# A two-layer DeltaNet/Conformer encoder on one core: gate tiles two ahead, splits two to a place, transposes in groups 1-2-1, the scan's last parts and the merge's operands in another order

## The chip, the core and the metric

The kernel runs on one NeuronCore of a Trainium2 chip. Five engines take part, each with its own instruction stream: TensorE (PE, matmuls and transposes into PSUM), VectorE (DVE, elementwise on PSUM and SBUF), ScalarE (ACT, functions by table, copies, squares), GpSimd (POOL) and SyncE (SP, which issues most DMAs; ACT and POOL issue some). [...] The metric is the time on the device of one launch, in microseconds (us), as the median of several runs; less is better.

## The reference

Two layers, each on x of 2048 tokens x 1024 channels (float32), then a final RMSNorm:

```
h = rms_norm(x, norm_w)
qkv, z_a, a_lg, b_lg, cf_val, cf_glu, z_b, gate_lg = split(h @ w_in)
q, k, v = silu(depthwise_conv5(qkv));  q, k = l2_normalize(q), l2_normalize(k)      # 4 heads of 128
o = delta_rule(q, k, v, g, beta) + flip(delta_rule(flip(q), ...))                   # 2 directions
o = o * rsqrt(mean(o*o) + EPS) * dn_norm_w * silu(z_a);  y_a = o @ w_dn_out
u = silu(layer_norm(depthwise_conv31(cf_val * sigmoid(cf_glu)) + cf_conv_b)) * silu(z_b)
y_b = u @ w_cf_out
gate = sigmoid(gate_lg + gate_b)                       # one gate of 1024 for each branch
x = x + (gate[0] * y_a + gate[1] * y_b) @ w_out
```

The delta rule is a scan in chunks: in each chunk a small triangular system, and from chunk to chunk a 128x128 state for each head and direction.

## The kernel before

Activations lie with channels on the 128 partitions and tokens along the free dimension. The 2048 tokens are four blocks of 512 (`blk` 0 to 3), two to a half. Every projection is made of denses: one output tile of 128 channels x 512 tokens in a PSUM bank (`pd`). Weights and operands are cut in a high and a low part by `split` (L158 on ACT copies the high part, L159 on DVE subtracts), and `dense_steps` (L175 to L177) runs three matmuls of 512 columns for each 128 input channels: 24 matmuls where the input has 1024 channels (w_in, w_out), 12 where it has 512 (w_cf, w_dn). Small results go to the five banks of `pz`.

A layer runs in four stages.

**Projections and heads.** `conv_tiles` makes the denses of two or three 128-channel columns of w_in and a five-tap convolution with SiLU (L546) for each half. Work that hangs on it is put in queues as Python generators and taken up between denses: `follow` lets a generator of `post` go on to its next `yield` after each dense, and `pump` does the same for `back` by a credit in us (a `yield 0.0` ends the pump for this dense). `keys` is a `post` generator: `token_major` turns 16 chunks of 128 tokens with PE transposes (L567), four to a pz bank and eight between two yields, the keys first, then the queries; ACT squares them (L595, L605) and copies the keys (L597). Then come the gram products of 16 chunks (L622, L623), copied by ACT (L625). `conformer_conv` is a 31-tap convolution on DVE (L734), a `back` generator, and `conformer_norm` (another, one for each blk) is the layer norm of branch B: sums over channels by PE, squares, a sum for each token (`token_sum`, L201), a reciprocal root, and a multiply. The string `Z` says how many empty pumps lie between its parts.

**Scan.** `delta` walks 16 steps, chunk `step` forward and chunk 15 - `step` backward in one pass, first half of the steps storing o, second half adding to it and closing the chunk with `finish` (squares L1028, reciprocal root on DVE from L1038 to L1042, scale by ACT L1046, transposes by PE L1051, product with z_a L1052, store of og). Its matmuls are short, so it pulls denses from a filler between its parts: `pull(n)` takes n pieces of three matmuls. The filler is the second half's gate columns (`gates(1)`, 256 pieces), then `early_merge`: branch B's products of half 0 (w_cf, 12 matmuls each), multiplied by the sigmoid of a gate tile (`g`) into `y1`. The operand `u` is loaded and split (tile `uop`) at given pieces: `SPLIT` is the first of eight pieces in a row. After the loop, `TAIL` gives the pulls between the last parts of `finish`. The order of the scan is bound as written (`bind`) on PE, ACT, DVE and POOL; elsewhere the tile framework schedules each engine's stream by priority and buffers.

**Merge.** For each half, 8 output tiles j and two blocks b: `gt` (a gate tile, in an `hm` buffer; two gates in half 1) is loaded and put through a sigmoid (L1227); in half 1 a dense with wc (w_cf) gives branch B, multiplied with the gate (L1232); a dense with wd (w_dn) over `og` gives branch A (L1235), the two are added (L1236) and split into yhi and ylo. In half 0 the operand `og` (tile `gop`) is loaded in four pieces of 1024 tokens when the scan ends; half 1's operands are loaded during half 0's output projection.

**Output.** w_out over yhi and ylo, residual, next layer's norm; in the last layer `last_out` with the final norm.

Of the kernel before, what the change touches and what calls it, by code (L numbers as in the profile page):

```python
# [6 lines left out]
F32 = mybir.dt.float32  # L7
F32R = mybir.dt.float32r
# [6 lines left out]
P = 128  # L15
# [4 lines left out]
KD = 8  # L20
# [7 lines left out]
GAP = 0  # L28
SPLIT = 247
LEAD = (8, 10, 6, 6, 6, 4)  # L30
STEP = (4, 4, 4, 4)
TAIL = (3, 3, 2)
Z = '121'
# [25 lines left out]
def sort(ps):  # L59
    return ps.rearrange("p (i a) -> p a i", a=2)  # L60


def cut(x):
    return x.rearrange("p (a i) -> p a i", a=2)
# [13 lines left out]
class Trunk:  # L78
# [482 lines left out]

    def token_major(self, src, f):
        for q in range(4):
            ps = self.pz()
            for i in range(4):
                c = 4 * q + i
                self.nc.tensor.transpose(ps[:, i * P:(i + 1) * P], src[:, c * P:(c + 1) * P], self.ident)  # L567
            f(q, ps)
            if q % 2:
                yield  # L570
# [15 lines left out]
    def keys(self, hd, kt, qt, vs):  # L586
# [5 lines left out]
        def k_out(q, ps):  # L592
            ko = self.st("ko")
            for i in range(4):
# [4 lines left out]
                       ko.rearrange("p (c e) -> p c e", e=P))  # L599
        yield from self.token_major(kt, k_out)  # L600
        self.store(self.kq_d[:, :, hd, 1, :].rearrange("c p t -> p c t"), qt.rearrange("p (c t) -> p c t", t=P))
        ssq = self.sm(16, "ssq")
        def q_out(q, ps):
            for i in range(4):
                nc.scalar.activation(self.junk, ps[:, i * P:(i + 1) * P], AF.Square,  # L605
                                     accum_out=ssq[:, 4 * q + i:4 * q + i + 1])
        yield from self.token_major(qt, q_out)
        rq = self.sm(16, "rq")
# [140 lines left out]
    def conformer_norm(self, blk):  # L749
# [23 lines left out]
        yield 4.0  # L773
        for _ in range(int(Z[1])):
            yield 0.0
# [42 lines left out]
    def delta(self):  # L818
# [272 lines left out]
        for step in range(NCH):  # L1091
# [25 lines left out]
            new = finish(list(done))  # L1117
            done.clear()
            next(new)
            pull(STEP[2])  # L1120
# [4 lines left out]
            ins = nxt  # L1125
        for n in TAIL:
            pull(n)
            next(last)
        for _ in fill:
# [3 lines left out]
    def filler(self):  # L1133
        wcf = self.a["w_cf"][self.l]
        u = None
        for n, v in enumerate(self.gates(1)):
            yield v
            if n == 30 * KD - 1:
# [4 lines left out]
                for b in range(2):  # L1143
                    for k in range(4):
                        self.load(raw(k, b).bitcast(F32), self.u_d[k, :, b * NB:(b + 1) * NB])
            if n == 31 * KD - 1:
                ahead = self.weight(wcf[0], 4)
            if SPLIT <= n < SPLIT + 8:
                b, k = divmod(n - SPLIT, 4)
                self.split(u[:, k, b * NB:(b + 1) * NB], raw(k, b), raw(k, b).bitcast(F32))  # L1150
        self.u0 = u
        self.y1 = self.big([P, KD, HALF], F32, "y1")
        yield from self.early_merge(wcf, ahead)

    def early_merge(self, wcf, ahead):
        nc = self.nc
        seq = [(j, b) for j in range(KD) for b in range(2)]

        def gate(i):
            j, b = seq[i]  # L1160
            t = self.st("g1")
            self.load(t, self.gt_d[8 + j][:, b * NB:(b + 1) * NB])
            return t
        nxt = gate(0)
        for i, (j, b) in enumerate(seq):
            if b == 0:
                wc = ahead
                if j + 1 < KD:
                    ahead = self.weight(wcf[j + 1], 4)
            g = nxt  # L1170
            if i + 1 < len(seq):
                nxt = gate(i + 1)
            nc.scalar.activation(g, g, AF.Sigmoid)
# [26 lines left out]
    def merge(self, l, xd, fnw):  # L1200
# [10 lines left out]
        for half in range(2):  # L1211
            if half == 0:
                og, piece = self.operands(self.og_d, 0, "gop")
                for k in range(4):
                    piece(k)
            yhi = self.big([P, KD, HALF], F32R, "yhi")
            ylo = self.big([P, KD, HALF], F32R, "ylo")
            for j in range(KD):
                wc = self.weight(a["w_cf"][l, j], 4) if half else None
                wd = self.weight(a["w_dn"][l, j], 4)  # L1220
                for b in range(2):
                    sl = slice(b * NB, (b + 1) * NB)
                    tk = slice(half * HALF + b * NB, half * HALF + (b + 1) * NB)
# [3 lines left out]
                    nc.scalar.activation(gt[:, 0:n], gt[:, 0:n], AF.Sigmoid)  # L1227
                    y = [gt[:, 0, :], gt[:, 1, :] if half else self.y1[:, j, sl]]
                    if half:
                        ps = self.pd()  # L1230
                        self.dense(ps, wc, lambda k: (u[:, k, sl], u[:, 4 + k, sl]), 4)
                        v_.tensor_tensor(out=cut(y[1]), in0=sort(ps), in1=cut(y[1]), op=ALU.mult)  # L1232
                    ps = self.pd()
                    self.dense(ps, wd, lambda k: (og[:, k, sl], og[:, 4 + k, sl]), 4)
# [8 lines left out]
            if last:  # L1243
                self.last_out(l, half, xd, fnw, yhi, ylo, ahead)
                continue
# [3 lines left out]
            for j in range(KD):  # L1249
# [10 lines left out]
                if j == 0:  # L1260
                    ss = self.hm("ss")[:, 0:HALF]
                for b in range(2):
                    sl = slice(b * NB, (b + 1) * NB)
# [30 lines left out]

    def last_out(self, l, half, xd, fnw, yhi, ylo, ahead):
        nc, a = self.nc, self.a
# [40 lines left out]

        for b in range(2):
            o = b * NB
# [111 lines left out]
```

## Time and profile before

| | us |
|---|---|
| median of three runs | 3188.68 (3188.55 to 3192.41) |
| the profiled execution's own time | 3190.01 |
| its span in the trace | 3188.2 |
| stage: projections and heads of layer 0 | about 100 to 800 |
| scan of layer 0 | about 800 to 1300 |
| merge and output of layer 0 | about 1300 to 1700 |
| layer 1, the same stages | 1700 to 2400, 2400 to 2860, 2860 to 3188 |

The profile names an instruction by its engine, its line in the kernel (L567), its operation and its tiles (output<-inputs, buffer numbers left out), then partitions x elements. In a timeline a row gives start, duration, and in brackets how long the engine had been idle before it and what it had waited for. Rows of the same kind in sequence are merged (x7). Durations of matmuls overlap; from start to start they show the pace. PEclk is the clock granted to PE as a share of full speed. DMA rows with SPq, ACTq or POOLq tell who issued them.

### The profile page before, as it was taken

How to read it: one execution, taken by the hardware profiler on the slowest of the kernel's cores; microseconds unless marked ns; L12 is line 12 of the kernel's file. 1: busy time of each engine (PE TensorE's matmuls, PEld its weight loads, DVE VectorE, ACT ScalarE, POOL GpSimd, SP SyncE). 2: the span in 40 equal slices, each digit the busy share in tenths (PEclk: the TensorE clock that was granted, in tenths of full speed). 3: DMA queues.
4: the chain of work that ended last, by engine and by line, in shares of the span. 5: the costliest groups of instructions: out<-in, count | busy, mean ns of one | idle time of the engine just before them, and what ended most of it. 6: DMA issues, size and time to landing. Idle time of an engine off the chain costs nothing. (4 is left out here: it accounts for less than half of the span.)

```text
span 3188.2 us, 51447 instructions
## 1 busy us (share of the span) xinstructions
PE 3095.3 (97%) x19190; PEld 2712.7 (85%) x19190; DVE 2400.1 (75%) x4433; ACT 1385.1 (43%) x3107; POOL 301.4 (9%) x297
## 2 busy tenths in 40 slices
PE   6999999999999999999999999999999999999998
PEld 5788888888889998787888888888888899978787
DVE  7789898987656697745676989898954567867665
ACT  5625151522444466533345242425234445655342
POOL 3000000000022231000000000000001213200000
PEclk9999999999999999999999999999999999999999
DMA  4332232334687886554413131313357878855643
GB/s 140 89 97 93 85 95 85 96 110 132 204 287 251 256 263 212 189 189 128 141 50 108 66 115 65 114 66 113 125 169 261 260 240 259 282 185 190 207 152 126
DMA packets 428266, 501.72 MB, mean 157 GB/s; under 512 B 96304, under 2 KB 262832, under 8 KB 428016
## 3 DMA queue, kind: packets, MB, share of 16 engines
q1 hardware_dynamic: 354688, 388.58, 39.2%
q10 hardware_dynamic: 65264, 80.09, 7.3%
q0 software_dynamic: 8064, 29.76, 2.5%
q8 instruction: 151, 2.47, 0.3%
q14 instruction: 99, 0.81, 0.1%
HBM read 342.74 MB, written 155.58 MB: 156 GB/s over the span
## 5 line engine op out<-in xcount | busy, mean ns | idle before, releaser
L175 PE MATMUL pd<-h,whi 128*128 128x512 f32 x2816 | 1091.8, 388 | 0.0
L177 PE MATMUL pd<-h,wlo 128*128 128x512 f32 x2816 | 1070.2, 380 | 2.2 <-DVE wlo L159 2.2
L176 PE MATMUL pd<-h,whi 128*128 128x512 f32 x2816 | 1071.3, 380 | 0.0
L734 DVE SCALAR_TENSOR_TENSOR cacc<-gp,vec,cacc 128x1009 f32<-128x1009 f32 (+1 forms) x480 | 614.5, 1280 | 37.8 <-ACT cacc L732 34.6
L175 PEld LDWEIGHTS pd<-h,whi 128*128 128x128 f32 x2816 | 534.1, 190 | 79.3 <-issue 1.4
L177 PEld LDWEIGHTS pd<-h,wlo 128*128 128x128 f32 x2816 | 533.9, 190 | 79.2 <-DVE wlo L159 3.8
L176 PEld LDWEIGHTS pd<-h,whi 128*128 128x128 f32 x2816 | 534.2, 190 | 72.4 <-issue 1.9
L158 ACT ACTIVATE whi<-wraw 128x512 fp32r<-128x512 f32 x394 | 239.1, 623 | 451.0 <-PE pd L176 325.4
L159 DVE TENSOR_TENSOR wlo<-wraw,whi 128x512 fp32r<-128x512 f32 x394 | 272.1, 704 | 133.4 <-ACT whi L158 133.0
L559 DVE SCALAR_TENSOR_TENSOR acc<-cin,vec,acc 128x1022 f32<-128x1022 f32 (+1 forms) x192 | 246.6, 1299 | 14.4 <-ACT acc L557 13.2
L177 PE MATMUL pd<-yhi,wlo 128*128 128x512 f32 x488 | 185.7, 381 | 3.8 <-DVE wlo L159 3.8
L175 PE MATMUL pd<-yhi,whi 128*128 128x512 f32 x488 | 185.5, 380 | 1.2 <-ACT whi L158 1.2
L176 PE MATMUL pd<-ylo,whi 128*128 128x512 f32 x488 | 185.0, 379 | 0.0
L814 ACT ACTIVATE go<-pd,vec 128x512 f32<-128x512 f32 x128 | 87.0, 680 | 145.7 <-PE pd L177 136.2
L535 ACT ACTIVATE cin<-pd 128x512 f32<-128x512 f32 x96 | 56.9, 593 | 154.9 <-PE pd L177 154.8
L746 ACT ACTIVATE ao<-pd 128x512 f32<-128x512 f32 x64 | 38.3, 598 | 170.0 <-PE pd L177 169.9
L175 PE MATMUL pd<-uop,whi 128*128 128x512 f32 x256 | 102.2, 399 | 7.1 <-ACT whi L158 7.1
L177 PEld LDWEIGHTS pd<-yhi,wlo 128*128 128x128 f32 x488 | 92.2, 189 | 19.2 <-DVE wlo L159 6.2
L175 PEld LDWEIGHTS pd<-yhi,whi 128*128 128x128 f32 x488 | 92.2, 189 | 15.0 <-ACT whi L158 2.3
L176 PEld LDWEIGHTS pd<-ylo,whi 128*128 128x128 f32 x488 | 92.2, 189 | 12.9
L177 PE MATMUL pd<-uop,wlo 128*128 128x512 f32 x256 | 99.5, 389 | 2.4 <-DVE wlo L159 1.7
L176 PE MATMUL pd<-gop,whi 128*128 128x512 f32 x256 | 98.2, 384 | 2.4 <-DVE gop L159 2.3
(311 smaller groups left out, 4837.1 us busy)
## 6 DMA issues: line engine op xcount, KB each, us to landing
wraw<-w_in SPq DMA_DIRECT2D x240, 256.0 KB, 3.3
gt<-go ACTq DMA_DIRECT2D x128, 256.0 KB, 3.6
dl<-gr SPq DMA_DIRECT2D x128, 256.0 KB, 5.1
dl<-kq SPq DMA_DIRECT2D x64, 512.0 KB, 6.3
dl<-kv SPq DMA_DIRECT2D x64, 512.0 KB, 5.6
wraw<-w_out SPq DMA_DIRECT2D x90, 256.0 KB, 3.1
kq<-acc SPq DMA_DIRECT2D x16, 1024.0 KB, 5.4
gr<-go ACTq DMA_DIRECT2D x64, 256.0 KB, 2.2
```

What stands on the lines that cost most here:

```text
L158: self.nc.scalar.activation(hi, src, AF.Copy)
L159: self.nc.vector.tensor_tensor(out=lo, in0=src, in1=hi.bitcast(F32), op=ALU.subtract)
L175: mm(ps, whi[:, k, :], xhi, start=k == 0, stop=False)
L176: mm(ps, whi[:, k, :], xlo, start=False, stop=False)
L177: mm(ps, wlo[:, k, :], xhi, start=False, stop=k == kk - 1)
L535: nc.scalar.activation(cut(t[:, o + b * NB:o + (b + 1) * NB]), sort(ps), AF.Copy)
L559: self.nc.vector.scalar_tensor_tensor(out=out, in0=t[:, k:k + n], scalar=wc(k), in1=out, op0=ALU.mult, op1=ALU.add)
L734: self.nc.vector.scalar_tensor_tensor(out=acc, in0=t[:, k:k + n], scalar=wc(k), in1=acc, op0=ALU.mult, op1=ALU.add)
L746: nc.scalar.activation(cut(o), sort(ps), func)
L814: nc.scalar.activation(cut(o), sort(ps), AF.Identity, bias=self.vec[:, V_GB + j:V_GB + j + 1])
```

## The change

Seven edits, letters as they are used below.

- **A.** `token_major` takes the places of its yields as an argument; keys and queries yield after the first and third bank. The groups of the heads become [k0], [k1, k2], [k3, q0], [q1, q2], [q3 and the gram products of chunks 0 to 7], [gram, chunks 8 to 15], where they were [k0, k1], [k2, k3], [q0, q1], [q2, q3], [gram], [gram].
- **B.** One more empty pump before the token sum of blk 3 in `conformer_norm`.
- **C.** u's eight splits at pieces 245 to 258, two to a pull, in place of eight pieces from 247.
- **D.** The gate tiles of `early_merge`: two are loaded before it begins, and each round issues the load of the tile after next.
- **E.** The scan's last parts: the loop ends after the last squares, and the two open `finish` generators go on in the order new, last, new, new, new with 2, 2, 1, 3, 4 pieces ahead.
- **F.** og's half 0 in eight pieces of 512 tokens, block 1 first; the merge, w_out and `last_out` of half 0 take block 1 first.
- **G.** In half 1 of the merge, wc's denses of both blocks come before wd's of both; the gate tiles of both blocks are loaded and put through the sigmoid ahead.

```diff
-SPLIT = 247
+SPLITS = (245, 247, 249, 251, 253, 255, 257, 258)
-TAIL = (3, 3, 2)
+TAIL = (2, 2, 1, 3, 4)
...
-    def token_major(self, src, f):
+    def token_major(self, src, f, cuts=(1, 3)):
...
-            if q % 2:
+            if q in cuts:
                 yield
...
-        yield from self.token_major(kt, k_out)
+        yield from self.token_major(kt, k_out, (0, 2))
...
-        yield from self.token_major(qt, q_out)
+        yield from self.token_major(qt, q_out, (0, 2))
...
-        for _ in range(int(Z[1])):
+        for _ in range(int(Z[1]) + (blk == 3)):
             yield 0.0
...
             new = finish(list(done))
             done.clear()
+            if step == NCH - 1:
+                break
             next(new)
...
-        for n in TAIL:
+        for n, part in zip(TAIL, (new, last, new, new, new)):
             pull(n)
-            next(last)
+            next(part)
...
+        seq = [(j, b) for j in range(KD) for b in range(2)]
+        u = ahead = None
+        gs = deque()
+
+        def gate(i):
+            j, b = seq[i]
+            t = self.st("g1")
+            self.load(t, self.gt_d[8 + j][:, b * NB:(b + 1) * NB])
+            gs.append(t)
...
+                gate(0)
             if n == 31 * KD - 1:
                 ahead = self.weight(wcf[0], 4)
-            if SPLIT <= n < SPLIT + 8:
-                b, k = divmod(n - SPLIT, 4)
+                gate(1)
+            if n in SPLITS:
+                b, k = divmod(SPLITS.index(n), 4)
                 self.split(u[:, k, b * NB:(b + 1) * NB], raw(k, b), raw(k, b).bitcast(F32))
...
-            g = nxt
-            if i + 1 < len(seq):
-                nxt = gate(i + 1)
+            if i + 2 < len(seq):
+                gate(i + 2)
+            g = gs.popleft()
...
-                og, piece = self.operands(self.og_d, 0, "gop")
-                for k in range(4):
-                    piece(k)
+                og = self.big([P, 8, HALF], F32R, "gop")
+                for b in (1, 0):
+                    c = slice(b * NB, (b + 1) * NB)
+                    for k in range(4):
+                        self.load(og[:, 4 + k, c].bitcast(F32), self.og_d[k, :, c])
+                        self.split(og[:, k, c], og[:, 4 + k, c], og[:, 4 + k, c].bitcast(F32))
...
+            order = (0, 1) if half else (1, 0)
             for j in range(KD):
+                ys = {}
...
-                for b in range(2):
-                    sl = slice(b * NB, (b + 1) * NB)
+                for b in order:
...
-                    y = [gt[:, 0, :], gt[:, 1, :] if half else self.y1[:, j, sl]]
-                    if half:
+                    ys[b] = [gt[:, 0, :], gt[:, 1, :] if half else self.y1[:, j, b * NB:(b + 1) * NB]]
+                if half:
+                    for b in order:
+                        sl = slice(b * NB, (b + 1) * NB)
+                        y = ys[b]
                         ps = self.pd()
                         self.dense(ps, wc, lambda k: (u[:, k, sl], u[:, 4 + k, sl]), 4)
                         v_.tensor_tensor(out=cut(y[1]), in0=sort(ps), in1=cut(y[1]), op=ALU.mult)
+                for b in order:
+                    sl = slice(b * NB, (b + 1) * NB)
+                    y = ys[b]
                     ps = self.pd()
                     self.dense(ps, wd, lambda k: (og[:, k, sl], og[:, 4 + k, sl]), 4)
...
-                for b in range(2):
+                for b in order:
```

The lines of the kernel after this change are shifted: L1173, L1179, L1227, L1232, L1235 and L1236 of before are L1181, L1187, L1239, L1247, L1253 and L1254 after.

On PE, in the second head of layer 0, the transposes (L567) stand between matmuls of the values' denses. Before:

```order
L177 MATMUL pd<-h_107,wlo 128x512
L567 MATMUL pz<-con,acc 128x128 x7
L175 MATMUL pd<-h_231,whi 128x512
...
L175 MATMUL pd<-h_231,whi 128x512
L567 MATMUL pz<-con,acc 128x128
L176 MATMUL pd<-h_231,whi 128x512
```

Ten matmuls lie between the seventh transpose and the eighth, where the scheduler put it. After the change:

```order
L177 MATMUL pd<-h_107,wlo 128x512
L567 MATMUL pz<-con,acc 128x128 x4
L175 MATMUL pd<-h_231,whi 128x512
...
L177 MATMUL pd<-h_231,wlo 128x512
L567 MATMUL pz<-con,acc 128x128 x8
```

The first group ends after four, and the eighth transpose stands in the group one dense of 24 matmuls later.

On ACT, step 14 of the scan in layer 0: u's splits (uop), the squares and the first gates. Before:

```order
L158 ACTIVATE uop<-uop 128x512 x4
L814 ACTIVATE go<-pd,vec 128x512
L152 DMA gt_150<-go 128x512
L947 ACTIVATE dh_6989<-pz 128x256
L909 ACTIVATE dh_6988<-dh_6988 32x4x32 x4
L1028 ACTIVATE junk,oss<-dm_6984 128x128 x8
L158 ACTIVATE whi<-wraw 128x512
L1173 ACT_TABLE_LOAD
L1173 ACTIVATE g_11059<-g_11059 128x512
L1173 ACTIVATE g_11067<-g_11067 128x512
L982 ACTIVATE dm_6983<-pz,eg 128x128 x8
```

After:

```order
L158 ACTIVATE uop<-uop 128x512 x2
L814 ACTIVATE go<-pd,vec 128x512
L152 DMA gt_150<-go 128x512
L947 ACTIVATE dh_6989<-pz 128x256
L909 ACTIVATE dh_6988<-dh_6988 32x4x32 x4
L1028 ACTIVATE junk,oss<-dm_6984 128x128 x8
L158 ACTIVATE uop<-uop 128x512
L158 ACTIVATE whi<-wraw 128x512
L1181 ACT_TABLE_LOAD
L1181 ACTIVATE g_10748<-g_10748 128x512
L158 ACTIVATE uop<-uop 128x512 x2
L1181 ACTIVATE g_10896<-g_10896 128x512
```

Two of the four splits ahead of the squares are gone from there (they come a place earlier), and three that stood earlier still now lie behind the squares, two of them between the two gates.

On DVE, half 1 of the merge, one round of j. Before:

```order
L1232 TENSOR_TENSOR gt<-pd,gt 128x512
L159 TENSOR_TENSOR ylo<-gt,yhi 128x512
L159 TENSOR_TENSOR wlo<-wraw,whi 128x512
L1235 TENSOR_TENSOR gt<-pd,gt 128x512
L159 TENSOR_TENSOR wlo<-wraw,whi 128x512
L1236 TENSOR_TENSOR gt<-gt 128x512
L159 TENSOR_TENSOR ylo<-gt,yhi 128x512
L1232 TENSOR_TENSOR gt<-pd,gt 128x512
L1235 TENSOR_TENSOR gt<-pd,gt 128x512
L1236 TENSOR_TENSOR gt<-gt 128x512
```

After:

```order
L1247 TENSOR_TENSOR gt<-pd,gt 128x512 x2
L159 TENSOR_TENSOR wlo<-wraw,whi 128x512
L1253 TENSOR_TENSOR gt<-pd,gt 128x512
L1254 TENSOR_TENSOR gt<-gt 128x512
L159 TENSOR_TENSOR ylo<-gt,yhi 128x512
L1253 TENSOR_TENSOR gt<-pd,gt 128x512
L159 TENSOR_TENSOR wlo<-wraw,whi 128x512
L1254 TENSOR_TENSOR gt<-gt 128x512
L159 TENSOR_TENSOR ylo<-gt,yhi 128x512
```

The two subtractions of weights (wlo), which stood close together around one multiply, now stand four operations apart, and both multiplies of branch B come first.

More of the change, by code (lines that the diff above doesn't have):

```diff
@@ L1134, in filler, with units @@
         wcf = self.a["w_cf"][self.l]
-        u = None
-        for n, v in enumerate(self.gates(1)):
+        seq = [(j, b) for j in range(KD) for b in range(2)]
[6 more added lines that the diff above has]
+            gs.append(t)
+        def units():
+            yield from self.gates(1)
+            self.u0 = u
+            self.y1 = self.big([P, KD, HALF], F32, "y1")
+            yield from self.early_merge(wcf, ahead, seq, gs, gate)
+        for n, v in enumerate(units()):
             yield v
@@ L1145, in filler, with early_merge @@
                         self.load(raw(k, b).bitcast(F32), self.u_d[k, :, b * NB:(b + 1) * NB])
+                gate(0)
             if n == 31 * KD - 1:
                 ahead = self.weight(wcf[0], 4)
-            if SPLIT <= n < SPLIT + 8:
-                b, k = divmod(n - SPLIT, 4)
+                gate(1)
+            if n in SPLITS:
+                b, k = divmod(SPLITS.index(n), 4)
                 self.split(u[:, k, b * NB:(b + 1) * NB], raw(k, b), raw(k, b).bitcast(F32))
[L1151 to L1155, printed above, removed]
+    def early_merge(self, wcf, ahead, seq, gs, gate):
         nc = self.nc
[L1157 to L1164, printed above, removed]
         for i, (j, b) in enumerate(seq):
@@ L1243, in merge @@
             if last:
-                self.last_out(l, half, xd, fnw, yhi, ylo, ahead)
+                self.last_out(l, half, xd, fnw, yhi, ylo, ahead, order)
                 continue
@@ L1293, in late_norm, with last_out @@
         yield from self.normalise(1, xn, r, wcol)
-    def last_out(self, l, half, xd, fnw, yhi, ylo, ahead):
+    def last_out(self, l, half, xd, fnw, yhi, ylo, ahead, order):
         nc, a = self.nc, self.a
@@ L1336, in run @@
                     return
-        for b in range(2):
+        for b in order:
             o = b * NB
```

## The prediction

> **What bounds the kernel now.** First the busy times on the page of the profile:
>
> ```profile
> PE 3095.3 (97%) x19190; PEld 2712.7 (85%) x19190; DVE 2400.1 (75%) x4433; ACT 1385.1 (43%) x3107; POOL 301.4 (9%) x297
> ```
>
> TensorE (PE) is busy for 97% of the span, DVE for three quarters, ACT for less than half. The change removes no matmul, so all it can win or lose is time in which PE stands still or runs at a lower clock. The table of what PE waited for (total us, times, longest) says where that is:
>
> ```profile
> PE pz L567 <- ACT acc L546: 8.9, 6, 1.6
> PE pz L973 <- DVE dh L1052: 8.4, 2, 4.2
> PE pz L201 <- DVE lnt L772: 5.5, 4, 1.9
> PE pd L176 <- DVE gop L159: 2.3, 3, 0.8
> PE pz L1051 <- ACT dm L1046: 2.2, 2, 1.1
> PE pd L175 <- ACT gop L158: 1.0, 2, 0.8
> ```
>
> Most edits of the change stand beside one of these rows. A stall can cost more than its idle time. The table of windows (length; busy time and count of each engine; granted PE clock; DMA share; GB/s) shows stretches at half clock:
>
> ```profile
> 1235.60:1239.00 3.40, 2.46 (x11) 2.46 (x12) 3.35 (x8) 1.05 (x5) 1.27 (x1) 0.50 0.63 200
> 1303.90:1307.30 3.40, 3.27 (x8) 2.63 (x9) 3.40 (x5) 2.72 (x5) 0.00 (x0) 0.50 0.87 328
> 1454.10:1457.50 3.40, 3.40 (x8) 2.62 (x9) 2.70 (x6) 1.05 (x2) 0.00 (x0) 0.50 0.48 91
> 2420.00:2423.40 3.40, 3.40 (x9) 2.68 (x10) 2.74 (x16) 0.00 (x0) 0.00 (x0) 0.51 0.63 204
> 2846.70:2850.10 3.40, 3.40 (x10) 2.77 (x10) 2.10 (x3) 2.24 (x4) 0.00 (x0) 0.50 0.85 280
> ```
>
> A window of 3.4 us at clock 0.50 does the work of 1.7 us, so it costs **1.7 us**; all five follow a stall.
>
> **A, the heads' transposes in groups 1-2-1.** In heads 1 to 3 the eighth key transpose reads columns that the second half's SiLU writes:
>
> ```profile
> 281.08 0.33 PE L567 MATMUL pz<-con,acc 128*128 128x128 f32 x1 [1.56 <-ACT acc L546]
> ```
>
> That is one of six (8.9 us in all, three heads, two layers). With four transposes in the first group, the eighth comes one whole dense later: 24 matmuls, and two starts of 512 columns lie 0.216 us apart (rows below), so 5.2 us against a wait of 1.4 to 1.6. Term **-8.9**. What could be late next: the fifth group holds four transposes and four gram matmuls, all five pz banks at once. ACT empties it with four squares and four copies; the wait table names no wait of PE for a pz that ACT's copies free, and ACT is idle for 57%. ACT also gets three more table loads, 1.28 us each (row below), 3.8 us under the same cover; without it they would be paid. Bounds -10 to -5.
>
> **B, one pump later for block 3.** Four of the eight token sums (L201) waited; the fourth of each layer is block 3:
>
> ```profile
> 861.15 1.05 PE L201 MATMUL pz<-con,lnt 128*128 128x1 f32 x8 [1.31 <-DVE lnt L772]
> 2418.93 1.05 PE L201 MATMUL pz<-con,lnt 128*128 128x1 f32 x8 [1.37 <-DVE lnt L772]
> ```
>
> One dense (5.2 us) more covers both: -1.3 -1.4, and the half-clock window at 2420.0 goes with the second, -1.7. Term **-4.4** (bounds -4.4 to -2.7); the two waits of block 2 stay.
>
> **C, u's splits two to a place.** The largest stall is at step 14 of the scan, once in each layer. A matmul waits for the pz that L1052 frees; L1052 stands on DVE behind a multiply with a sigmoid, and that on ACT behind a table load:
>
> ```profile
> 1221.82 2.50 DVE L159 TENSOR_TENSOR uop<-uop 128x512 fp32r<-128x512 f32 x4 [2.33 <-ACT uop L158]
> ...
> 1233.18 1.28 ACT L1173 ACT_TABLE_LOAD   x1
> 1234.47 1.15 ACT L1173 ACTIVATE g<-g 128x512 f32<-128x512 f32 x2
> ...
> 1235.74 1.40 DVE L1052 SCALAR_TENSOR_TENSOR dh<-pz,vec,dh 128x512 f32<-128x512 f32 x2
> 1236.54 0.80 PE L973 MATMUL pz<-dh,dl 128*128 128x128 f32 x2 [4.21 <-DVE dh L1052]
> ```
>
> Four splits ahead of this chain become two: the chain starts 2 x 0.62 = 1.25 us earlier, and the whi split could begin at 1231.3. But in the new order three splits move inside it, one ahead of whi, two between the first sigmoid and L1052. ACT: split 0.55, whi 0.6, table 1.3, sigmoid 0.6 end at 1234.4, two splits at 1235.5; DVE: the last subtraction 0.65, the multiply 0.6, L1052 0.7, so about 1237.5 against 1236.5. The stall is not removed but 1.0 us longer in each layer: **+2**. Bounds: -15 (both stalls of 4.2 us and two windows of 1.7 in each layer gone) to +6 (a further window each).
>
> **D, gate tiles two ahead.** No row of PE's waits names the gate tile g. SP issues each load now after one earlier multiply has freed its buffer, with weights and og stores queued behind. Bounds 0 to +3.4 in each layer (one 256 KB load held back, row below); I take **0**, the value of the wait table.
>
> ```profile
> g<-gt SPq DMA_DIRECT2D x32, 256.0 KB, 3.4
> ```
>
> **E, the scan's tail.** Before, 36 matmuls lie between the last two groups of L1051, now 24, so PE comes 2.6 us earlier to transposes that wait for this chain (last two rows: the wait table of each layer's tail, 1240 to 1300 and 2798 to 2860):
>
> ```profile
> 1283.89 0.16 DVE L1038 TENSOR_TENSOR oss<-oss,cq 128x8 f32<-128x8 f32 x1
> ...
> 1286.37 0.17 DVE L1042 TENSOR_TENSOR orr<-orr,cq 128x8 f32<-128x8 f32 x1
> 1287.03 2.38 PE L1051 MATMUL pz<-con,dm 128*128 128x128 f32 x8 [1.10 <-ACT dm L1046]
> PE pd L175 <- ACT whi L158: 1.0, 1, 1.0
> PE pd L175 <- ACT whi L158: 0.4, 1, 0.4
> ```
>
> The fourteen DVE operations take 2.65 us. In the new order a multiply and a weight subtraction no longer stand ahead of them, but four og splits (0.52 us each on ACT) are mixed with the squares: squares end near 1281.2, DVE's chain at 1284.4, L1051 starts near 1285.0. PE is there at 1281.9, so it waits 3 us in place of 1.1 and the whi wait (1.0 and 0.4). Net +0.5 and +1.0, and a half-clock window in layer 0, where there was none: **+3.2**. Bounds -5.3 (all these waits and the window at 2846.7 gone) to +6.6.
>
> **F, og by block, the finished one first.**
>
> The wait table's two gop rows, 2.3 and 1.0 us, are the start of the merge in both layers, where og's tiles are still landing (row of the DMA issues: count, size, median us to landing):
>
> ```profile
> gop<-og SPq DMA_DIRECT2D x16, 512.0 KB, 6.3
> ```
>
> Block 1 of half 0 needs none of the last chunks; block 0 is wanted a half dense after block 1, and five more denses lie behind the last L1051. The 3.3 us and layer 0's window at 1303.9 (1.7) go: **-5.0**. Four more DMAs per layer on SP; each 256 KB piece is bounded by the 6.3 us of the 512 KB ones, within the 15 us of cover (6 denses of 12 matmuls, 2.6 us each). Bounds -5.0 to 0.
>
> **G, weights for two blocks in half 1.** PE alternates wc and wd for each block; the whi split stands on ACT behind the sigmoid of a gate tile that has just landed:
>
> ```profile
> 1451.69:1454.05 2.36, 0.17 (x2) 0.00 (x1) 0.54 (x1) 2.15 (x4) 0.00 (x0) 1.00 0.00 0
> 1454.05:1511.53 57.48, 55.35 (x241) 45.80 (x241) 32.42 (x51) 21.64 (x31) 0.00 (x0) 0.97 0.48 138
> 3003.00:3045.00 42.00, 37.36 (x167) 30.62 (x166) 25.70 (x41) 14.91 (x21) 0.00 (x0) 1.00 0.50 159
> 1451.90 1.06 ACT L1227 ACTIVATE gt<-gt 128x1024 f32<-128x1024 f32 x1 [5.47 <-DMA gt<-gt]
> L1235 DVE TENSOR_TENSOR gt<-pd,gt 128x512 f32<-128x512 f32 x64 | 43.9, 686 | 20.8 <-PE pd L177 20.8
> gt<-gt SPq DMA_DIRECT2D x32, 512.0 KB, 5.0
> PE pd L177 <- DVE wlo L159: 1.7, 2, 1.1
> 1450.83 0.38 PE L177 MATMUL pd<-gop,wlo 128*128 128x512 f32 x1
> 1451.04 0.38 PE L175 MATMUL pd<-gop,whi 128*128 128x512 f32 x1
> ```
>
> The last two rows give the pitch, 0.21 to 0.22. So 241 matmuls need 52.1 us and took 57.5; with the 2.2 before them layer 0 loses 7.6, and layer 1 42.0 - 36.1 = 5.9. Now a split is wanted two denses (5.2 us) later than the one before. What binds next is the tile's round: a new tile needs a buffer that the split ylo of the third tile before frees. In the new order: load 5.0, sigmoid 1.06, yhi 0.63, ylo 0.69, three DVE operations 2.1, yhi 0.63, ylo 0.69 = 10.8 us per j, against 48 x 0.216 = 10.4 on PE. The lag, 0.4 x 7 = 2.8 us, has three pd banks and 5.2 us of slack to go into. I take -7.0 (bounds -7.6 to -4.8) and in layer 1, where DVE's two early waits of 1.7 (the wlo row, window 2990 to 3050) stay, -4.3: **-11.3**.
>
> **Sum:** -8.9 - 4.4 + 2 + 0 + 3.2 - 5.0 - 11.3 = -24.4. The profiled execution took 3190.0 us (span 3188.2 and 1.8 around it): 3165.6. It lies 1.3 above the median of the runs, 3188.7, so I forecast **3164**.
>
> [...]
>
> **Rivals.** (1) *Waits only move*: half 1 stays at the pace of its gate tiles, so G gives just the first wait and little more, -3, and both late chains come out at +3 and +4.7 a pair: -8.9 - 4.4 + 6 + 4.7 - 5.0 - 3 = -10.6, 3178. For it: the round of 10.8 is as long as PE's; against it: the bounded lag. Chance 0.22. (2) *The step-14 stall and the tail go too*: -8.9 - 4.4 - 15 - 5.3 - 5.0 - 11.3 = -50, 3139. For it: the chain does start 1.25 us earlier; against it: three splits inside. Chance 0.12. (3) *Half-clock windows come regardless of these stalls*, on the next wait: the 1.7 of B, F and G and the 1.7 of E are taken out, -24.4 + 5.1 - 1.7 = -21.0, 3168; the longest L201 wait, 1.9 us, has none behind it, which speaks for it; the five rows speak for the forecast. Chance 0.05. (4) *Slower*: in half 1 of layer 0 both tiles of a j are held from load to last ylo. If only two buffers rotate, load and sigmoid no longer overlap the denses and j takes 10.8 + 5.2 = 16 us, 7 x (16 - 11.5) = +32 in place of -7: -24.4 + 39 = +14.6, 3203. It decides from a round of 11.5 + 27/7 = 15 us on. Against it: layer 0 has three such buffers (the hm tiles that the next norm does not hold). Chance 0.04. (5) *It does not do what it says*: the order shows all parts moved, but each freed wait may fall to the next producer: within 6 us of before. Chance 0.06. The forecast keeps 0.51.
>
> **Numbers.** The range takes the forecast with its bounds, (1), (3) and the upper part of (2): 3146 to 3181. 0.2% is 6.4 us, about what a measurement can tell from no change. Faster: 0.51 + 0.18 of (1) + 0.12 + 0.05 = 0.86; same: 0.04 of (1) and 0.05 of (5): 0.09; slower: 0.04 + 0.01 = 0.05.
>
> **What would show it.** Right: no row "L567 <- L546" in PE's waits, two L201 rows for lnt in place of four, no wait for gop at the start of the merge, j of half 1 at 10.4 to 10.6 us; the wait for L1052 still there at about 5 us. Wrong: a wait for L1052 under 2 us (rival 2), a j of 11 us or more with a wait for whi or yhi (1), PE waits for pz behind L625 in the heads (A), or for g in the scan (D).

## The result and the profile after

| | before | after |
|---|---|---|
| median of six runs, us | 3190.57 (3188.55 to 3193.55) | 3174.82 (3171.55 to 3178.22) |
| ratio of after to before | | 0.9949, 95% interval 0.9937 to 0.9962 |
| profiled execution, us | 3190.01 | 3171.55 |
| its span, us | 3188.2 | 3169.8 |

The change is faster by 15.8 us. The forecast was 3164 (3146 to 3181), 24.4 faster: the direction and the range held, a third of the gain is missing. In the two profiled executions the difference is 18.4. The table cuts it at instructions that both traces have (start of the first one of each stage, after minus before, layer 0 and layer 1).

| stretch | layer 0 | layer 1 | sum | forecast |
|---|---|---|---|---|
| heads, first transposes to block 0's token sum (A) | -4.5 | -5.8 | -10.4 | -8.9 |
| block 2's sum to the scan's second step (B) | +3.4 | +2.1 | +5.5 | -4.4 |
| scan, to the first dense of u (D) | 0.0 | 0.0 | 0.0 | 0 |
| step 14, to the last output product L989 (C) | +1.3 | +2.9 | +4.2 | +2 |
| tail and start of the merge (E, F) | -3.5 | -0.7 | -4.3 | +3.2 - 5.0 |
| half 1 of the merge (G) | -7.1 | -6.7 | -13.8 | -11.3 |
| all the rest | | | +0.2 | |

So two terms miss: B with the wrong sign, by 9.9, and C by 2.2; A, G and the pair E and F each brought 1.5 to 2.5 more than forecast. The small rest hides a loss: layer 1's output of half 0 is 3.1 longer (1.7 of it the half-clock window at 2907.0, behind a wait of 1.7 for a weight subtraction, wlo), and the other pieces are 2.9 shorter together.

The page of the profile after, busy times, and then the table of what PE waited for (total us, times, longest):

```profile
PE 3088.8 (97%) x19190; PEld 2713.7 (86%) x19190; DVE 2399.9 (76%) x4441; ACT 1387.1 (44%) x3118; POOL 298.9 (9%) x297
```

```profile
PE pz L214 <- DVE dg L212: 14.9, 7, 3.5
PE pd L175 <- ACT uop L158: 9.6, 4, 3.4
PE pz L1051 <- ACT dm L1046: 6.7, 2, 3.9
PE pz L201 <- DVE lnt L772: 2.5, 2, 1.9
PE pz L567 <- ACT go L625: 0.4, 1, 0.4
```

Read against the table of before: the six waits of the transposes for L546 (8.9 us) are gone, a single one of 0.4 for L625 is there; the lnt waits went from four to two; the waits for L1052 (8.4) and for gop (3.3) are gone. Three others stand in their place. The spread of block 3's root over the partitions (L214) waits for DVE in both layers, and L214's row grew from 8.7 to 14.9; the denses of u wait for their own operand (uop, 9.6); and the transposes L1051 wait 6.7 where they waited 2.2.

The table of windows of after (length; PE, PEld, DVE, ACT, POOL busy and counts; granted clock; DMA share; GB/s), with the stretches at half clock between 100 and 3150 us and one stretch of half 1:

```profile
831.70:835.10 3.40, 3.40 (x10) 2.77 (x10) 2.74 (x16) 0.00 (x0) 0.00 (x0) 0.50 0.60 194
1231.10:1237.90 6.80, 5.54 (x17) 3.96 (x17) 4.92 (x9) 2.96 (x5) 0.00 (x0) 0.50 0.35 110
1285.70:1289.10 3.40, 3.40 (x10) 2.61 (x11) 2.38 (x4) 2.03 (x5) 0.00 (x0) 0.50 0.43 155
1437.50:1495.50 58.00, 58.00 (x271) 50.78 (x270) 35.81 (x56) 22.93 (x33) 0.00 (x0) 1.00 0.53 146
2415.50:2418.90 3.40, 3.40 (x11) 2.68 (x10) 2.29 (x1) 0.88 (x2) 0.00 (x0) 0.50 0.00 0
2777.30:2784.10 6.80, 5.33 (x17) 4.44 (x18) 5.02 (x10) 2.44 (x5) 0.00 (x0) 0.50 0.47 142
2831.90:2835.30 3.40, 3.40 (x11) 2.53 (x11) 1.67 (x3) 2.74 (x8) 0.00 (x0) 0.51 0.23 77
2907.00:2910.40 3.40, 3.40 (x9) 2.68 (x9) 3.40 (x5) 2.00 (x3) 0.00 (x0) 0.50 0.69 199
```

Half 1 of the merge now runs 271 matmuls in 58.0 us, 0.214 each, at full clock: PE waits for nothing there. The half-clock windows moved with the stalls: those at 1303.9 and 1454.1 are gone; those at 831.7, 1285.7 and 2907.0 are new, and two in a row begin at 2777.3 in layer 1's step 14, where before has one (2795.5).

### The profile page after: what moved, and what is told of

The parts are those of the page before. It is cut to its first block, busy times and chain, and to the rows that moved or that the text cites. A ratio compares the mean times of both kernels' runs of the same rounds, so it can differ in the third digit from the quotient of the medians.

```text
span 3169.8 us, 51513 instructions
## 1 busy us (share of the span) xinstructions
PE 3088.8 (97%) x19190; PEld 2713.7 (86%) x19190; DVE 2399.9 (76%) x4441; ACT 1387.1 (44%) x3118; POOL 298.9 (9%) x297
## 5 line engine op out<-in xcount | busy, mean ns | idle before, releaser
L559 DVE SCALAR_TENSOR_TENSOR acc<-cin,vec,acc 128x1022 f32<-128x1022 f32 (+1 forms) x192 | 246.3, 1299 | 14.8 <-ACT acc L557 13.7
L175 PE MATMUL pd<-uop,whi 128*128 128x512 f32 x256 | 101.8, 398 | 9.6 <-ACT uop L158 9.6
L175 PEld LDWEIGHTS pd<-yhi,whi 128*128 128x128 f32 x488 | 92.5, 190 | 14.8 <-ACT whi L158 2.0
L176 PE MATMUL pd<-uop,whi 128*128 128x512 f32 x256 | 99.7, 390 | 0.5 <-DVE uop L159 0.5
```

Of the source, the lines that this page charges most:

```text
L175: mm(ps, whi[:, k, :], xhi, start=k == 0, stop=False)
L176: mm(ps, whi[:, k, :], xlo, start=False, stop=False)
L559: self.nc.vector.scalar_tensor_tensor(out=out, in0=t[:, k:k + n], scalar=wc(k), in1=out, op0=ALU.mult, op1=ALU.add)
```

## The experiments

All ratios are to the kernel before, run beside it on the same chip: four or five timed runs of each changed kernel (eleven of the one with F alone) and nine or fifteen of before.

**Two theories for B.** Moved by a dense, block 3's token sum no longer waits, but its reciprocal root (DVE, L780 to L212) falls into the start of the scan. The first theory: it is slowed there by POOL, which adds masks to the scan's first matrices (L891). The second: it stands in DVE's order behind two weight subtractions (wlo) that wait for late weights. DVE and POOL of after, layer 0 (start, duration, engine, line, tiles; in brackets the idle time before and what ended it):

```profile
862.44 1.26 DVE L193 TENSOR_SCALAR rsv<-lv 128x4 f32<-128x4 f32 x1
863.72 1.78 DVE L159 TENSOR_TENSOR wlo<-wraw,whi 128x512 fp32r<-128x512 f32 x1
865.42 1.23 DVE L195 TENSOR_TENSOR rst<-lr,rsv 128x4 f32<-128x4 f32 x1
866.69 1.19 DVE L196 TENSOR_TENSOR rst<-rst,lr 128x4 f32<-128x4 f32 x1
...
869.77 0.87 DVE L212 TENSOR_SCALAR dg<-con,lr 128x128 f32<-128x128 f32 x4
```

```profile
862.36 2.59 POOL L891 TENSOR_TENSOR dm<-dm,con 128x512 f32<-128x512 f32 x2 [12.32 <-DMA dm<-gc]
865.17 2.68 POOL L891 TENSOR_TENSOR dm<-dm,con 128x512 f32<-128x512 f32 x2 [0.22 <-DMA dm<-gc]
```

The same operations in before, where POOL's first mask addition began at 867.6, after the root's end:

```profile
862.52 0.16 DVE L193 TENSOR_SCALAR rsv<-lv 128x4 f32<-128x4 f32 x1
862.71 0.16 DVE L195 TENSOR_TENSOR rst<-lr,rsv 128x4 f32<-128x4 f32 x1
...
864.48 0.88 DVE L212 TENSOR_SCALAR dg<-con,lr 128x128 f32<-128x128 f32 x4
```

Operations of 128x4 took 0.16 us in before, and three of them 1.19 to 1.26 in after while POOL added masks. The root took 3.1 us in before (862.24 to 865.36) and 8.5 in after (862.16 to 870.64). In layer 1 of after both are at work: DVE waits 2.9 us for the high parts of two weights (whi), and two operations of the root are slow beside POOL.

```profile
2407.93 0.69 DVE L159 TENSOR_TENSOR wlo<-wraw,whi 128x512 fp32r<-128x512 f32 x1 [1.73 <-ACT whi L158]
...
2410.28 0.69 DVE L159 TENSOR_TENSOR wlo<-wraw,whi 128x512 fp32r<-128x512 f32 x1 [1.20 <-ACT whi L158]
2410.89 1.22 DVE L195 TENSOR_TENSOR rst<-lr,rsv 128x4 f32<-128x4 f32 x1
```

*Without B.*

```diff
-        for _ in range(int(Z[1]) + (blk == 3)):
+        for _ in range(int(Z[1])):
```

> The changed kernel without edit B (block 3's token sum at its old place). Theory: B did not remove a wait, it handed it on. In the changed kernel PE waits for the spread (L214) behind block 3's token sum, 2.7 us in layer 0 and 3.5 in layer 1, where before it waited 1.3 and 1.4 for the sum itself. Without B the two L214 waits are gone, two L201 waits of 1.3 come back, and by the program's marks block 3 to the scan's first step is 1.5 to 2 us shorter in each layer: the kernel is 3 to 4 us (0.1%) faster than the changed one, ratio to before 0.9935 to 0.994. Rival (the forecast's B was right, and what is missing lies elsewhere): without B the kernel is 3 to 4 us slower than the changed one, ratio 0.996.

Measured: 3168.67, ratio 0.9928 (0.9916 to 0.9941). The L214 wait is gone, but the two waits of 1.3 for the sum did not come back: in layer 0 block 3's sum has no wait at all, in layer 1 it has one that is longer than in before (1.4):

```profile
PE pz L201 <- DVE lnt L772: 3.1, 1, 3.1
```

In layer 0 a half-clock window (831.7 to 835.1) holds PE up by 1.7 us ahead of the sum, more than the 1.3 that it waited in before. In layer 1 the tile that the block's norm loads came later. DVE's wait for it, without B and then in before:

```profile
2381.52 0.69 DVE L759 TENSOR_TENSOR lnt<-lnc 128x512 f32<-128x512 f32 x1 [5.11 <-DMA lnc<-cv]
2401.56 0.69 DVE L759 TENSOR_TENSOR lnt<-lnc 128x512 f32<-128x512 f32 x1 [3.44 <-DMA lnc<-cv]
```

Without B the rest of the change is 6.2 us faster by the medians; the intervals of the two ratios just overlap. So B most likely cost time, and the waits that it was to cover were no longer the 1.3 and 1.4 of before.

*The masks of the scan's first step on DVE.* The computation is the same on another engine.

```diff
-                nc.gpsimd.tensor_tensor(out=gb, in0=gb, in1=msk[:, None, :].to_broadcast([P, 4, P]), op=ALU.add)
+                (nc.gpsimd if step else v_).tensor_tensor(out=gb, in0=gb, in1=msk[:, None, :].to_broadcast([P, 4, P]), op=ALU.add)
```

> The changed kernel with the two mask additions of the scan's first step (L891) on DVE, where they stand behind the reciprocal root, and not on POOL; the order of DVE's root of block 3 stays as it is, two weight subtractions inside. Theory 1 (DVE's small operations take 1.1 to 1.3 us in place of 0.16 while POOL adds the masks): the root from L780 to the last L212 falls from 8.1 to about 4.4 us in layer 0 and from 9.3 to about 7 in layer 1; the L214 wait behind block 3's sum is gone in layer 0 and at most 1.5 in layer 1; 3 to 6 us faster than the changed kernel in all, half-clock windows included. Theory 2 (the root is late because weight subtractions and their loads stand inside it): the root stays at 7 us or more in both layers, the L214 waits stay at 2.5 to 3.5, no gain.

Measured: 3169.78, ratio 0.9935 (0.9921 to 0.9948). The next step's two additions still ran on POOL beside the root; two of its operations were slow (1.24 and 1.20), and the root of layer 0 took 7.1. The waits of PE for it, layer 0 (840 to 900 us) and layer 1 (2400 to 2440):

```profile
PE pz L214 <- DVE dg L212: 1.3, 1, 1.3
PE pz L214 <- DVE dg L212: 4.4, 1, 4.4
```

In layer 0 the wait halved; in layer 1 it didn't shrink. That left the two theories undivided, so the next run took all mask additions out of the way.

*The masks of the first two steps on DVE.*

```diff
-                (nc.gpsimd if step else v_).tensor_tensor(
+                (nc.gpsimd if step > 1 else v_).tensor_tensor(
```

> The changed kernel with the mask additions of the scan's first two steps on DVE, behind the reciprocal root; moving those of step 0 alone left the two of step 1 on POOL and two stretched operations in the root. Theory 1 (POOL's additions stretch DVE's small operations): no operation of the root over 0.3 us beside the two weight subtractions; the root from L780 to the last L212 takes 4.4 to 5.5 us in layer 0 and the L214 wait there is under 0.5. Theory 2 (weight subtractions inside the root, waiting for late loads): the root stays at 6.5 us or more in layer 1, where DVE waits for whi in it, and the L214 wait there stays at 2 or more. Both can hold, one in each layer.

Measured: 3166.66, ratio 0.9922 (0.9908 to 0.9935). No POOL instruction runs in either stretch, and no small operation of the root is slow. In layer 0 the root takes 4.85 us (863.50 to 868.35) and PE's wait for it is gone. In layer 1 it takes 10.0 and PE waits 4.2 us all the same:

```profile
PE pz L214 <- DVE dg L212: 4.2, 1, 4.2
```

DVE there:

```profile
2408.20 0.69 DVE L159 TENSOR_TENSOR wlo<-wraw,whi 128x512 fp32r<-128x512 f32 x1 [3.63 <-ACT whi L158]
...
2411.45 0.69 DVE L159 TENSOR_TENSOR wlo<-wraw,whi 128x512 fp32r<-128x512 f32 x1 [2.09 <-ACT whi L158]
...
2413.24 0.87 DVE L212 TENSOR_SCALAR dg<-con,lr 128x128 f32<-128x128 f32 x4
```

In layer 0 POOL's additions make the wait. In layer 1 the root stands 3.63 + 2.09 = 5.7 us behind two weight subtractions that wait for ACT, and ACT for weights that SP issues among the loads of the scan's first matrices; with POOL out of the way the root only waits longer for them (5.7 us in place of 2.9). That the weights come late because of that place among SP's loads is read from the trace (in after, SP issues the two at 2403.19 and 2404.15, between the scan's loads that begin at 2402.77 and 2404.57, and ACT waits 5.77 and 1.15 us for them); moving them was not tried.

The stretch of the table from block 2's sum to the scan's second step says the same. Its length against before, less 1.7 us for each half-clock window in it:

| | after | after, run again (below) | masks of step 1 on DVE | masks of steps 1 and 2 on DVE | without B |
|---|---|---|---|---|---|
| layer 0 | +1.7 | +1.6 | +0.8 | -1.5 | -1.6 |
| layer 1 | +2.1 | +2.4 | +3.1 | +2.8 | +1.4 |

By these traces, one of each kernel, B cost 3.3 us in layer 0, and taking POOL's additions away gives all of it back. In layer 1 it cost some 0.7 to 1.0, and taking them away gives nothing. The medians of the two runs with masks on DVE, 5 and 8 us below after, are lower than this stretch accounts for; the rest of their gain is not assigned.

**C: when must u's splits be done?** In after the wait at step 14 is not for L1052 any more. ACT and then PE of after, layer 0:

```profile
1229.43 0.61 ACT L158 ACTIVATE uop<-uop 128x512 fp32r<-128x512 f32 x1
1229.95 0.61 ACT L158 ACTIVATE whi<-wraw 128x512 fp32r<-128x512 f32 x1
1230.58 1.28 ACT L1181 ACT_TABLE_LOAD   x1
1231.88 0.63 ACT L1181 ACTIVATE g<-g 128x512 f32<-128x512 f32 x1
1232.41 1.13 ACT L158 ACTIVATE uop<-uop 128x512 fp32r<-128x512 f32 x2
```

```profile
1230.10 0.48 PE L175 MATMUL pd<-uop,whi 128*128 128x512 f32 x1 [3.42 <-ACT uop L158]
1233.08 0.80 PE L175 MATMUL pd<-uop,whi 128*128 128x512 f32 x1 [1.26 <-ACT uop L158]
1236.10 1.92 PE L973 MATMUL pz<-dh,dl 128*128 128x128 f32 x8
```

The splits that moved back are operands of the dense that stands ahead of L973. It waits first for the split behind the eight squares, then for one behind the sigmoid, 4.7 us together, and two windows at half clock begin 1.0 us after the first wait (1231.1 to 1237.9). One run put the splits where they were, one put all eight earlier.

*Splits as before.*

```diff
-SPLITS = (245, 247, 249, 251, 253, 255, 257, 258)
+SPLITS = (247, 248, 249, 250, 251, 252, 253, 254)
```

> The changed kernel with u's splits where they were (pieces 247 to 254). Theory: C moved the step-14 stall from the pz that L1052 frees to the operand itself, since the second uop dense waits for splits that stand behind the squares on ACT; by the marks step 14 cost 1.3 us more in layer 0 and 2.9 in layer 1. Without C: no PE wait for uop (9.6 us in four now), the L1052 wait of about 4.2 us is back in both layers, 3 to 4 us faster than the changed kernel in all. Rival (the table load binds, and C only adds 1.0 a layer by the splits inside the chain): 2 us faster. Rival (C helped): slower.

Measured: 3170.77, ratio 0.994 (0.9927 to 0.9952). No wait for uop, and the old one is back with its old length:

```profile
PE pz L973 <- DVE dh L1052: 8.5, 2, 4.2
```

Against after the intervals leave open whether C itself cost anything (0.9940 against 0.9949): one wait took the place of another of nearly its size. By the traces step 14 is 1.4 and 1.6 us shorter than in after.

*Splits earlier.*

```diff
-SPLITS = (245, 247, 249, 251, 253, 255, 257, 258)
+SPLITS = (243, 244, 245, 246, 247, 248, 249, 250)
```

> The changed kernel with u's splits four pieces earlier than before the change (243 to 250), so that all eight lie ahead of step 14. Theory (the chain of step 14 starts with L1001 on DVE behind the splits): four subtractions fewer ahead of L1001, so L1052 ends about 2 us earlier than in the kernel before; the wait for L1052 falls from 4.2 to 2 to 3 us, and no wait for uop: 5 to 8 us faster than the changed kernel, more if the half-clock windows of step 14 go. Rival (the squares on ACT and the table load bind, whatever stands ahead of L1001): the wait stays at 4.2, gain as without C, 3 to 4 us. Rival (u's loads have not landed at piece 243, ACT waits for them and holds up the scan): waits for ACT in step 13, no gain.

Measured: 3159.98, ratio 0.9905 (0.9888 to 0.9922). The wait, and ACT behind the squares:

```profile
PE pz L973 <- DVE dh L1052: 4.0, 2, 2.0
```

```profile
1227.07 0.61 ACT L158 ACTIVATE whi<-wraw 128x512 fp32r<-128x512 f32 x1
1227.70 1.28 ACT L1181 ACT_TABLE_LOAD   x1
```

The kernel of the run before is the one to compare with, since PE waits for L1052 in both. Without the four subtractions ahead of L1001 (DVE; 2.50 us for the four) the whole chain moves forward: counted from the first dense of u, the squares start at 3.6 us in place of 5.8 and the table load at 7.6 in place of 9.8. The wait falls by the same 2.2, from 4.2 to 2.0 in each layer, and no window at half clock follows it. Step 14 is 4.9 and 3.6 us shorter than in before, 3.4 and 1.7 of it the half-clock windows that are gone. So this chain ends the stall of before, and moving the splits forward shortens it; C moved three of them the other way.

**The other parts alone or taken out.** *A alone* (the yields of the transposes, nothing else):

```diff
-            if q % 2:
+            if q in cuts:
...
-        yield from self.token_major(kt, k_out)
+        yield from self.token_major(kt, k_out, (0, 2))
```

> The kernel before with edit A alone (transposes in groups 1-2-1). Theory (the term of the forecast, -8.9): no L567 wait for L546 in PE's waits; heads of layer 0 about 4.5 us shorter and of layer 1 about 5.8 (the marks of the changed kernel); ratio 0.9965 to 0.9975. Rival (A's gain in the changed kernel is partly other edits' or the phase of half-clock windows): under 6 us in the two stages together, ratio above 0.998.

Measured: 3176.73, ratio 0.9965 (0.9952 to 0.9978), the heads shorter by 4.6 and 5.8.

*G alone* (both blocks' products with wc ahead of both with wd, half 0 as before):

```diff
-                for b in range(2):
...
+                if half:
+                    for b in order:
+                        self.dense(ps, wc, lambda k: (u[:, k, sl], u[:, 4 + k, sl]), 4)
...
+                for b in order:
                     self.dense(ps, wd, lambda k: (og[:, k, sl], og[:, 4 + k, sl]), 4)
```

> The kernel before with edit G alone (half 1 of the merge: wc of both blocks, then wd of both; og and block order as before). Theory 1 (the weight split behind the gate's sigmoid was the whole loss of half 1): both halves 1 run without a wait of PE, 7.1 us shorter in layer 0 and 6.7 in layer 1, ratio 0.9955 to 0.996. Theory 2 (the forecast's: the tile's round of 10.8 us per j against 10.4 on PE stays as a small loss): 4 to 6 us in layer 0, waits for whi or yhi late in half 1.

Measured: 3170.49, ratio 0.9938 (0.9926 to 0.9951), half 1 shorter by 8.1 and 6.7, and PE waits for nothing in it. The median is 18.8 us below before, 4 more than half 1 accounts for.

*F alone* (og in pieces of 512 tokens, block 1 first):

```diff
-                og, piece = self.operands(self.og_d, 0, "gop")
...
+                for b in (1, 0):
+                    for k in range(4):
+                        self.load(og[:, 4 + k, c].bitcast(F32), self.og_d[k, :, c])
```

> The kernel before with edit F alone (og of half 0 by block, block 1 first in half 0). Theory: the gop waits at the start of the merge go in both layers with the half-clock window of layer 0: 4.3 us in layer 0 and 1 to 2 in layer 1; ratio 0.998 to 0.9985. Rival (F needs E, whose order puts the last og stores one dense earlier): PE still waits 1 us or more for gop of block 0 or at the first piece, gain under 3 us. A second rival: block 1 first in the last layer's half 0 costs time in its output (3.1 us longer in the changed kernel): then layer 1's gain is gone.

Measured: 3191.69, ratio 1.0001 (0.9992 to 1.001). The gop waits are gone, but PE now waits in each tail for a weight split. The wait rows of 1200 to 1300 and of 2750 to 2860, and ACT in the first of these:

```profile
PE pd L175 <- ACT whi L158: 2.5, 1, 2.5
PE pd L175 <- ACT whi L158: 3.4, 1, 3.4
```

```profile
1276.04 1.88 ACT L158 ACTIVATE gop<-gop 128x512 fp32r<-128x512 f32 x3 [1.45 <-DMA gop<-og]
...
1278.12 0.61 ACT L158 ACTIVATE gop<-gop 128x512 fp32r<-128x512 f32 x1
...
1281.53 0.61 ACT L158 ACTIVATE whi<-wraw 128x512 fp32r<-128x512 f32 x1
```

The four early splits of block 1 (2.4 us) stand ahead of and among the squares, the weight split behind them. All the same the stretch of tail and merge is 3.7 us shorter than in before in layer 0; in layer 1 it is 2.3 longer. What takes the gain back lies elsewhere too: layer 1's output of half 0 grew by 2.5, as the second rival has it (with A or G alone it grew by 1.0 and 1.3), and half 1 by 2.0 and 1.9. In layer 1's half 1 a half-clock window of 1.7 (3034.9) is new; what makes the 2.0 was not followed up.

*Without E* (the tail as before, all else changed):

```diff
-TAIL = (2, 2, 1, 3, 4)
+TAIL = (3, 3, 2)
...
-            if step == NCH - 1:
-                break
...
-        for n, part in zip(TAIL, (new, last, new, new, new)):
-            pull(n)
-            next(part)
+        for n in TAIL:
+            pull(n)
+            next(last)
```

> The changed kernel without edit E (the loop's end and the pulls of the tail as before). Theory: E lets PE come to the last transposes (L1051) 2.6 us too early, 2.8 and 3.9 us of wait with a half-clock window each; without E the wait is 1.1 in both layers and the tail 0.7 to 1.5 us shorter in each: 1.5 to 3 us faster than the changed kernel, ratio near 0.994. Rival (E is what keeps the gop waits away): without E PE waits for gop at the merge's start, 2 us or more, and the kernel is slower than the changed one.

Measured: 3175.14, ratio 0.9955 (0.9943 to 0.9968), the same as after. Without E the weight-split waits are 2.4 and 2.8 and the L1051 waits 1.1 and 0; with E there is no weight-split wait, and the L1051 waits are 2.8 and 3.9. E trades one for the other.

**The change again, and what the findings give together.** *After, unchanged,* for the spread between chips:

> The changed kernel once more, beside the other three. Theory and rival expect the same, 0.994 to 0.996 of before; it says how far one kernel's runs of two sessions differ, and so what a gap of 3 us between two kernels is worth. By the marks its step 14 is 1 to 3 us longer than before in each layer, and block 3's stretch 2 to 5.

Measured: 3175.21, ratio 0.9948 (0.9936 to 0.9961).

*Without B and with the early splits* (the two edits shown above):

> The changed kernel without B and with u's splits at pieces 243 to 250: the two repairs together. Theory (they lie in different stages and add up): 21 us less than the changed kernel by the two runs alone (6 and 15), 3153 to 3157, ratio 0.988 to 0.990; no wait for uop, L1052 waits of 2 us, no L214 wait at block 3. Rival (a good part of the two gains was the phase of the half-clock windows): 3160 to 3166, no better than the splits alone.

Measured: 3154.94, ratio 0.9886 (0.9872 to 0.9899), the lowest median of all, some 20 us below after and as expected. The L1052 waits are 2.7 each, not 2.

*Before with A, G and the splits from 243 on, without B, D, E and F:*

```diff
-SPLIT = 247
+SPLIT = 243
```

> The kernel before with A, with G and with u's splits four pieces earlier in a row (243 to 250); B, D, E and F left out. Theory (D, E and F give little: by the marks E and F together 4 us, F alone nothing): 3 to 5 us slower than the changed kernel without B and with the same splits, 3157 to 3162. Rival (E and F are worth nothing, since F's og splits on ACT delay the tail's weights as much as they save at the merge): equal to it within 2 us.

Measured: 3156.69, ratio 0.9891 (0.9877 to 0.9904). It equals the run before within the intervals: D, E and F together are worth nothing that these runs can tell.

## Why the prediction was right in direction and two thirds of the size

**B is the step that failed.** "One dense (5.2 us) more covers both: -1.3 -1.4, and the half-clock window at 2420.0 goes with the second, -1.7. Term -4.4." The first half came true: both waits of block 3's sum are gone. What was left out is the work behind the moved sum. It was costed as a place on PE alone; the root that follows on DVE moved too, to where POOL adds masks and where DVE's order holds weight subtractions. PE waited 2.7 and 3.5 us at L214 where it had waited 1.3 and 1.4 at L201: +3.5 where -4.4 stood, and a window came back at 2415.5. By the runs, POOL's additions make the whole cost in layer 0; in layer 1 DVE's late weights hold the root, and B itself cost little there. The other 1.7 of that stretch in layer 0 is the window at 831.7, behind block 2's wait; it came in the run without B as well. The bounds given for this term, -4.4 to -2.7, had no positive end at all. Rows of before would have given one: its root ran from 862.24 to 865.36 and POOL's additions from 867.60 to 873.24, so a root 5.2 us later falls beside them.

**C: the size and the reason.** Forecast +2, measured +4.2, of which 1.7 is the second half-clock window in layer 1. That the stall would stay was right, and rival 2, by which it would go, was wrong for this change. Its -15 was too large besides: before has two windows in step 14 of layer 0 and one in layer 1, so 13.5 is all that there was to win. The working of L1052 came out: counted from the first dense of u it starts 1.06 us later, 1.0 was forecast. But the forecast followed the three moved splits only as time ahead of L1052 on ACT and DVE; that they are operands of the dense ahead of L973 was not looked at, and there PE stood. With the splits from 243 to 250 the forecast's own chain (squares, weight split, table load, sigmoid, multiply, L1052) is what PE waits for.

**A** was right in its reason and 1.5 short: the L546 waits went, and the waits that came (0.7 at 295.5, 0.4 for L625, 0.7 at 1842.8) stayed under the bounds. Alone it gave 0.35%, and the heads were shorter by the same amount as in the whole.

**G** was right and 2.5 short. In layer 0 -7.0 was forecast and -7.1 measured. In layer 1 two early waits of 1.7 were taken to stay; they went. The tile's round of 10.8 us set no pace: rival 1 and the slower rival 4 fell with it.

**D** has no wait row before or after, 0 as forecast.

**E and F.** L1051's waits are 2.8 and 3.9 where 3.0 each was forecast, with a window each, and the gop waits went: the two traces give -4.3 where -1.8 was forecast. E's net was added up wrongly: a wait of 3.0 in place of 1.1 and 1.0 in layer 0, and of 1.1 and 0.4 in layer 1, is +0.9 and +1.5, not +0.5 and +1.0; the traces have +0.7 and +2.4. The timed runs don't confirm a gain of the two. F alone gave 0 where -5.0 was forecast: the gop waits went, but waits for the tail's weight split came, and half 1 and layer 1's output grew. Taking E out gave 0; and A, G and the early splits without D, E and F are as fast as with them. In the trace of A alone, which has neither E nor F, the same stretch is 1.9 shorter in layer 0 and 0.9 longer in layer 1, so a good part of what one trace shows in favour of E and F may be chance.

**Rival 3, windows that come regardless,** had a chance of 0.05 and was nearer than that: of the windows taken to vanish (1303.9, 1454.1, 2420.0) the first two went, but the third came back at 2415.5, 831.7 and 2907.0 are new, and step 14 of layer 1 has one more. Counting windows between 100 and 3150 us, before had seven and after nine, 2 x 1.7 = 3.4 us.

**The sum.** That it came as near as it did is partly luck: B, C and the rest missed by 12.4 us one way, A, G and the pair E and F by 6.4 the other. Alone, A and G give 12.6 and 18.8 us by the medians, 31 together, while the whole change gives 15.8; each ratio has an interval of about 4 us to either side. By the marks of the table A's and G's own stretches are 10.5 and 14.8 shorter when they run alone, 24.2 together in the whole change; the rest of the 31 lies where they change nothing (step 14 of layer 0 is 1.2 shorter in both traces, with one half-clock window where before has two). So the other five parts cost some 6 us by the trace, up to 15 by the medians. Undoing B gives back 6, undoing C 4, E and F nothing, each with such an interval; more is not assigned.

## What to carry to other kernels

When a step is moved to cover a wait, follow what hangs on it: here the sum on PE was early enough, and the twelve operations of 128x4 behind it came to lie beside another engine's work in one layer and, in the other, behind two subtractions with late inputs as well. When splits or copies are moved out of the way of a chain, look first at who reads them, and when. And a part that looks good in one trace should be run alone: two parts carried the gain, and the other five together gave some of it back.

## What the runs showed of the hardware

In after a short DVE operation lasted until the POOL operation beside it ended. The L193 that began at 862.44, just after POOL's first mask addition (862.36; 1.3 us, half of its pair's 2.59), ended at 863.70; the L196 from 866.69 ended at 867.88, and POOL's second pair ended at 867.85. With the masks of both steps on DVE the same operations took 0.16 us. Each of four operations in a row took 1.0 to 1.1 us more beside POOL, whatever its size: three of 128x4 1.26, 1.23 and 1.19 in place of 0.16, and the subtraction of 128x512 1.78 in place of 0.69. Not every operation did: the L787 of 128x2048 at 870.78 in before lay beside POOL's additions too and took 2.27 us, as all eight of its kind did (2.275 to 2.282). Why some last longer and others don't was not shown. The trace names no wait of DVE for POOL there: in this kernel the delay lies in the operations' own durations.

In these traces a stall of one length has a half-clock window behind it in one kernel and none in the other. Block 2's sum in layer 0 waited 1.89 us in before, and the clock stayed at 1.00 (836.5 to 840.0); in after it waited 1.88, and the window at 831.7 followed, 3.4 us at 0.50. A term of 1.7 us that hangs on one window is therefore a chance, not a cost; single runs of one kernel spread over up to 11.7 us (3155.29 to 3166.99, the splits from 243 on).
